# Strassen's seven products for five of eight pairs of contraction blocks in the feed-forward rounds of an encoder layer, in place of three

## The chip, the core and the metric

The kernel runs on one core of a Trainium2 chip. Five engines matter: TensorE (PE in the profile; its weight loads are PEld), VectorE (DVE), ScalarE (ACT), GpSimd (POOL) and SyncE (SP), whose queue issues the loads from memory. The metric is the device time of one execution in microseconds, lower is better. All data is 32-bit floating point.

## What is computed

One layer of an encoder on 256 tokens of width 2048: a feed-forward half, a mixing half (attention and a Fourier branch, gated), and a second feed-forward half. The change touches the two feed-forward halves alone:

```python
D_MODEL = 2048; SEQ = 256; D_FF = 5632

def _swiglu(x, w_gate, w_up, w_down):
    return (jax.nn.silu(x @ w_gate) * (x @ w_up)) @ w_down

def _macaron_ffn(x, pre_g, w_gate, w_up, w_down, post_g):
    return x + MACARON_WEIGHT * _rms_norm(_swiglu(_rms_norm(x, pre_g), w_gate, w_up, w_down), post_g)
...
    h = _macaron_ffn(h, ffn1_pre_g[l], ffn1_w_gate[l], ffn1_w_up[l], ffn1_w_down[l], ffn1_post_g[l])
    h = _gated_mixers(h, ...)
    h = _macaron_ffn(h, ffn2_pre_g[l], ffn2_w_gate[l], ffn2_w_up[l], ffn2_w_down[l], ffn2_post_g[l])
```

## The kernel before

**Precision by three products.** A 32-bit product is made of three passes of TensorE: every operand is split into a rounded part and its remainder. `split` (L102, L103) does that: ScalarE writes the rounded part `hi` by a copy, VectorE writes `lo = src - hi`. `mm3` (L107 to L109) then multiplies hi by hi, hi by lo and lo by hi into one PSUM tile. So each weight element that comes from memory costs ScalarE one element of copy, VectorE one of subtraction, and TensorE three passes for each of the two 128-token tiles.

**Rounds.** The 5632 columns of the feed-forward are 11 blocks of 512 (`f` = 0 to 10). The first two are made by `col_block`. For `f` = 2 to 10 there is one `swiglu` call each, 9 in each of the two halves, 18 in all: the gate and the up product of the block, both 256 x 512 with the 2048 contraction in 16 blocks of 128, that is 8 pairs of blocks. Between them stand the `row_line` calls, which multiply an earlier block's 256 x 512 result by `w_down` and add it to the row tiles `y` (two tiles of 128 x 2048, taken 512 columns at a time: `cb` = 0 to 3). A round, as the word is used here, is one `row_line` and the `swiglu` behind it.

**Strassen's form.** Seen as a 2 x 2 problem (two token tiles by gate and up, over a pair of contraction blocks), a pair costs eight block products, or seven by Strassen's way. A pair in the seven form needs sums of the token blocks (made once, in `Forms.chunk`) and sums of the weight blocks (made anew in every round, because the weights are new): in `seven`, four VectorE subtractions of 128 x 512 (`minus`, L538; two in `first`, then one in `first` behind a split, one in `second`). It feeds four pieces to TensorE: `rb` whole (2 products), `t` whole (2), `ra` whole (2), one half of `t` (1). A plain pair feeds two whole pieces (4 products each). In units of 128 x 1024 splits: 3.5 against 2. Each product is one `mm3`: 21 matmuls against 24. The products p1, p5, p6, p7 are common to several outputs and are added at the end by VectorE (`add`, L543) after ScalarE's `copy` (L547); then come `silu` (L551) and `times` (L555). In the kernel before, the three seven pairs are the first pairs of the first three chunks (`kg` = 0, 1, 2; a chunk is four contraction blocks), and the common products end with the third.

**Order.** The feed-forward rounds are scheduled by hand: VectorE, ScalarE and TensorE each keep program order. `Line.feed` keeps a queue of `RING` = 6 pieces: a piece's subtractions and split (`ready`) are issued when it enters, its matmuls (`use`) when six stand in the queue, and its additions (`then`) right behind its matmuls. So on VectorE a piece's additions stand ahead of the split of the sixth piece after it. The split pieces lie in a ring of six buffers, so the split of a piece waits until TensorE is done with the piece six before. Raw pieces (512 KB each) are loaded by SP's queue in order into `RAW_BUFS` = 5 buffers (L83); a load waits until its buffer's last reader is done.

**Buffers.** PSUM: five tiles `mm` (the accumulators u0, g0, g1, u1, p6, and two `pr` for each `cb` of a row line), three tiles `tr` (p1, p5, p7, and the transposes of `turn_h`, L177). `chunk` has three buffers under each of two names (the weight sums `t13`, and the transposed block results `hT`).

Of the kernel before, what the change touches and what calls it, by code (L numbers as in the profile page):

```python
# [10 lines left out]
F32 = mybir.dt.float32  # L11
# [37 lines left out]
BY_SEVEN = (0, 1, 2)  # L49
# [7 lines left out]
def encoder_layer(  # L57
# [371 lines left out]
    class Forms:  # L429
# [3 lines left out]
        def __init__(self, u, rs):  # L433
            self.u, self.rs, self.seven, self.plain = u, rs, {}, {}
            self.rooms = {}

        def room(self, n):

            for i, used in self.rooms.items():
                if used[0] + n <= D:  # L440
                    break
            else:
                i = len(self.rooms)
                used = self.rooms[i] = [0] + [big(f"f{c}{i}", F32R) for c in "hl"]
            used[0] += n
            return [a[:, used[0] - n:used[0]] for a in used[1:]]
# [11 lines left out]
        def chunk(self, kg):  # L458
# [6 lines left out]
            n = 0  # L465
            if kg in BY_SEVEN:
                n = 2
                f = chunk.tile([P, 7, P], F32, tag="ch_lo", name="sf")
                a11, a12, a21, a22 = a[:, 0, 0:P], a[:, 1, 0:P], a[:, 0, P:S], a[:, 1, P:S]
                A.activation(f[:, 0:2, :], a[:, 0:2, 0:P], AF.Copy)  # L470
                A.activation(f[:, 2, :], a22, AF.Copy, scale=-1.0)
                V.tensor_tensor(out=f[:, 3, :], in0=a21, in1=a22, op=ALU.add)
                V.tensor_tensor(out=f[:, 4, :], in0=f[:, 3, :], in1=a11, op=ALU.subtract)
                V.tensor_tensor(out=f[:, 5, :], in0=a11, in1=a21, op=ALU.subtract)
                V.tensor_tensor(out=f[:, 6, :], in0=a12, in1=f[:, 4, :], op=ALU.subtract)
                hi, lo = (x.rearrange("p (a b) -> p a b", b=P) for x in self.room(7 * P))
                split(hi, lo, f[:])
                self.seven[kg] = [(hi[:, i, :], lo[:, i, :]) for i in range(7)]
            hi, lo = (x.rearrange("p (a b) -> p a b", b=S) for x in self.room((CK - n) * S))
            split(hi, lo, a[:, n:, :])  # L480
            for k in range(n, CK):
                self.plain[kg * CK + k] = [(hi[:, k - n, t * P:(t + 1) * P], lo[:, k - n, t * P:(t + 1) * P]) for t in range(NT)]
# [35 lines left out]
    def swiglu(line, forms, w, hs):  # L518
# [10 lines left out]
        def plain(kg, i, c, ks, *then):  # L529
            def use(b):  # L530
                for t in range(NT):
                    for j, k in enumerate(ks):
                        mul(c + str(t), forms.plain[kg * CK + k][t], b[j], kg * CK + k == KD - 1)

            line.feed(lambda: ring(raw_piece(w[kg], i)[:]), use, *then)
# [22 lines left out]
        def seven(kg, end):  # L558
            a11, a12, na22, s1, s2, s3, s4 = forms.seven[kg]
            h = {}  # L560

            def first():
                ra, rb = raw_piece(w[kg], 0), raw_piece(w[kg], 1)
                t = chunk.tile([P, WP, NB], F32, tag=("ch_hi", "ch_lo")[kg % 2], name="t13")
# [12 lines left out]
            def two(n, a, m, b, last):  # L577
                def use(ws):
# [6 lines left out]
            plain(kg, 2, "g", (2, 3))  # L585
            line.feed(lambda: ring(h["ra"][:]), two("p1", a11, "p6", s2, end), *([copy, lambda: add("x2", "p6", "x1")] if end else []))
            line.feed(lambda: ring(h["t"][:, 0:1, :]), lambda ws: mul("g1", na22, ws[0]),
                      *([lambda: add("x3", "p7", "x2")] if end else []))
            plain(kg, 3, "u", (2, 3), *([lambda: add("x2", "p5", "x2")] if end else []))

        for kg in range(KD // CK):
            if kg in BY_SEVEN:
                seven(kg, kg == BY_SEVEN[-1])
                continue
            plain(kg, 0, "g", (0, 1), lambda: add("x5", "p5", "x3"))
            plain(kg, 1, "u", (0, 1))
            plain(kg, 2, "g", (2, 3), lambda: add("x1", "g0", "x1"), lambda: add("x3", "g1", "x3"),
                  lambda: silu(0), lambda: silu(1))
            plain(kg, 3, "u", (2, 3), lambda: add("x2", "u0", "x2"), lambda: times(0), lambda: add("x5", "u1", "x5"),
                  lambda: times(1))  # L600

    def row_line(line, ch, w, rb, y, first, ahead):

        for cb in range(D // NB):
            ps = []

            def use(b, i, cb=cb, ps=ps):
                if i == 0:
                    if cb == D // NB - 1:
                        ahead()  # L610
                    ps.extend(pmm.tile([P, NB], F32, tag="mm", name="pr") for _ in range(NT))
# [6 lines left out]
            def out(t, cb=cb, ps=ps):  # L618
                dst = cbs(y[t], cb)
                if first:  # L620
                    A.activation(dst, ps[t][:], AF.Copy)
                else:
                    V.tensor_tensor(out=dst, in0=ps[t][:], in1=dst, op=ALU.add)
# [5 lines left out]
    def ffn(u, rs, wg, wu, wgu, wd, yname, tail, gate0, w_next=None, early=()):  # L629
# [10 lines left out]
        for f in range(PLAIN):  # L640
# [19 lines left out]
        with tc.manual_schedule(engines={mybir.EngineType.DVE, mybir.EngineType.Activation, mybir.EngineType.PE}):  # L660
            for f in range(PLAIN, nblk + 1):
# [7 lines left out]
                row_line(line, chs[-1] if f > PLAIN else chs[0], wd, f - 2, y, f == PLAIN, ahead)  # L669
# [619 lines left out]
```

## Time and profile before

| | |
|---|---|
| median of three runs | 2040.54 us (2039.6 to 2041.2) |
| the profiled execution, its own time | 2041.46 us |
| its span from the first to the last instruction | 2039.7 us |
| TensorE busy | 2018.3 us, 99% of the span, 9308 matmuls |
| TensorE weight loads busy | 1673.0 us, 82% |
| VectorE busy | 1651.9 us, 81%, 2216 instructions |
| ScalarE busy | 1112.2 us, 55% |
| granted clock, mean | 0.999 of full speed |
| read from memory | 409.44 MB, 204 GB/s over the span |

A busy share is a mean over the whole span, and the feed-forward rounds are a regular stretch of it with shares of their own. A matmul of TensorE is counted from its start to its modelled end, and several are in flight at once, so its rate is read from the distance of two starts. The same holds for VectorE, where an instruction's end can lie behind the start of the next.

### The profile page before, as it was taken

The page shows a single profiled execution, that of the slowest core. Times are in us where ns is not written, and L with a number is a line of the kernel's source. Part 1 is how long each engine was busy: PE and PEld are TensorE (multiplying, and loading weights), DVE is VectorE, ACT ScalarE, POOL GpSimd, SP SyncE. Part 2 cuts the span into 40 slices and gives each one's busy share as a digit, 9 for nine tenths or more (in the row PEclk, how much of TensorE's full clock was granted, in tenths as well). Part 3 has the DMA queues.
Part 4 walks back from the last instruction along what each step waited for, and adds up shares of the span by engine and source line. Part 5 has one row for each costly group of instructions (what it writes and reads, how often), then busy time and mean ns, then how long its engine had stood idle before and what let it go on. Part 6 is the DMA issues. An engine that isn't in the chain of part 4 may idle for free.

```text
span 2039.7 us, 25718 instructions
## 1 busy us (share of the span) xinstructions
PE 2018.3 (99%) x9308; PEld 1673.0 (82%) x9308; DVE 1651.9 (81%) x2216; ACT 1112.2 (55%) x1490; POOL 50.9 (2%) x46
## 2 busy tenths in 40 slices
PE   9999999999999999999999999999999999999998
PEld 7888888888888878888888888788888888888886
DVE  6878888888888788887877895877788888888876
ACT  7554555544555556556666554555554555544553
POOL 0000000000000110100000000200000000000002
PEclk9999999999999999999999999999999999999999
DMA  8675566556666696964555557566665566656663
GB/s 315 212 271 178 190 218 205 193 175 201 209 207 190 208 294 194 271 187 138 192 190 188 183 179 276 186 207 225 220 203 173 192 218 204 196 174 198 211 209 106
DMA packets 118736, 417.43 MB, mean 205 GB/s; under 512 B 12968, under 2 KB 19120, under 8 KB 116432
## 3 DMA queue, kind: packets, MB, share of 16 engines
q1 hardware_dynamic: 114256, 411.66, 61.1%
q0 software_dynamic: 4352, 4.13, 1.4%
q8 instruction: 73, 1.20, 0.2%
q14 instruction: 55, 0.45, 0.1%
HBM read 409.44 MB, written 6.29 MB: 204 GB/s over the span
## 4 chain that ended last, share of the span: by engine, by line
PE 93%; DVE 4%; DMA 1%; ACT 1%; issue 0%; SPq 0%; DVEq 0%; ACTq 0%
PE pc L108 19%; PE pc L109 19%; PE pc L107 19%; PE pr L109 10%; PE pr L107 10%; PE pr L108 10%; PE pt L177 1%; DVE wlo L103 1%; DMA raw<-in_w_fo 1%; DVE h L390 0%; PE pe L107 0%; PE pe L109 0%; PE pe L108 0%; PE pt L976 0%; PE pf L109 0%
## 5 line engine op out<-in xcount | busy, mean ns | idle before, releaser
L102 ACT ACTIVATE whi<-raw 128x1024 fp32r<-128x1024 f32 (+1 forms) x711 | 749.0, 1059 | 618.8 <-PE pc L109 268.2
L103 DVE TENSOR_TENSOR wlo<-raw,whi 128x1024 fp32r<-128x1024 f32 (+1 forms) x711 | 860.5, 1220 | 277.1 <-ACT whi L102 271.4
L107 PE MATMUL pc<-whi,fh 128*128 128x512 f32 x1098 | 427.1, 389 | 0.0
L108 PE MATMUL pc<-wlo,fh 128*128 128x512 f32 x1098 | 427.1, 389 | 0.0
L109 PE MATMUL pc<-whi,fl 128*128 128x512 f32 x1098 | 427.1, 389 | 0.0
L107 PE MATMUL pc<-whi,uh 128*128 128x512 f32 x688 | 271.7, 395 | 0.2 <-ACT uh L698 0.2
L108 PE MATMUL pc<-wlo,uh 128*128 128x512 f32 x688 | 269.4, 392 | 2.3 <-DVE wlo L103 2.2
L109 PE MATMUL pc<-whi,ul 128*128 128x512 f32 x688 | 269.4, 392 | 1.5 <-DVE ul L103 1.5
L107 PE MATMUL pr<-whi,hTh 128*128 128x512 f32 x688 | 269.4, 392 | 0.0
L109 PE MATMUL pr<-whi,hTl 128*128 128x512 f32 x688 | 267.8, 389 | 0.0
L108 PE MATMUL pr<-wlo,hTh 128*128 128x512 f32 x688 | 267.7, 389 | 0.0
L107 PEld LDWEIGHTS pc<-whi,fh 128*128 128x128 f32 x1098 | 206.1, 188 | 42.8
L109 PEld LDWEIGHTS pc<-whi,fl 128*128 128x128 f32 x1098 | 206.1, 188 | 42.8
L108 PEld LDWEIGHTS pc<-wlo,fh 128*128 128x128 f32 x1098 | 206.1, 188 | 42.7
L109 PEld LDWEIGHTS pc<-whi,ul 128*128 128x128 f32 x688 | 129.4, 188 | 29.2 <-DVE ul L103 2.4
L108 PEld LDWEIGHTS pc<-wlo,uh 128*128 128x128 f32 x688 | 129.5, 188 | 28.9 <-DVE wlo L103 4.0
L107 PEld LDWEIGHTS pc<-whi,uh 128*128 128x128 f32 x688 | 129.5, 188 | 27.0 <-ACT uh L698 1.5
L109 PEld LDWEIGHTS pr<-whi,hTl 128*128 128x128 f32 x688 | 129.1, 188 | 26.9
L108 PEld LDWEIGHTS pr<-wlo,hTh 128*128 128x128 f32 x688 | 129.2, 188 | 26.1
L107 PEld LDWEIGHTS pr<-whi,hTh 128*128 128x128 f32 x688 | 129.2, 188 | 26.1
L102 ACT ACTIVATE whi<-t 128x1024 fp32r<-128x1024 f32 x108 | 90.9, 842 | 98.9 <-DVE t L538 44.5
L103 DVE TENSOR_TENSOR wlo<-t,whi 128x1024 fp32r<-128x1024 f32 x108 | 103.1, 954 | 15.6 <-ACT whi L102 15.6
(333 smaller groups left out, 2066.3 us busy)
## 6 DMA issues: line engine op xcount, KB each, us to landing
raw<-in_f_gu SPq DMA_DIRECT2D x288, 512.0 KB, 4.1
raw<-in_f_down SPq DMA_DIRECT2D x176, 512.0 KB, 5.0
raw<-in_w_in SPq DMA_DIRECT2D x112, 512.0 KB, 4.9
raw<-in_f_up SPq DMA_DIRECT2D x32, 512.0 KB, 4.7
raw<-in_w_ao SPq DMA_DIRECT2D x32, 512.0 KB, 4.0
raw<-in_w_out SPq DMA_DIRECT2D x32, 512.0 KB, 4.0
raw<-in_f_gate SPq DMA_DIRECT2D x31, 512.0 KB, 5.6
fraw<-in_w_f SPq DMA_DIRECT2D x16, 512.0 KB, 5.9
```

The lines of the kernel that those rows point to most:

```text
L102: a = A.activation(hi, src, AF.Copy)
L103: v = V.tensor_tensor(out=lo, in0=src, in1=hi.bitcast(F32), op=ALU.subtract)
L107: T.matmul(ps, lh, rh, start=first, stop=False)
L108: T.matmul(ps, lh, rl, start=False, stop=False)
L109: return T.matmul(ps, ll, rh, start=False, stop=last)
L177: T.transpose(pt[:, j, :], src[:, j * P:(j + 1) * P], ident[:])
```

## The change

Five pairs of the eight take the seven form: both pairs of the first chunk (0 and 1), and the first pair of the other three (2, 4 and 6). Pairs 3, 5 and 7 stay plain. With the last seven pair now in the last chunk, the common products are closed there, and their additions stand behind pair 6's third and fourth piece; the additions of gate and up stand behind the two pieces of pair 7 as they stood behind the last two pieces before. The order of the pieces in a round: in chunk 0 the eight pieces of two seven pairs; in chunks 1 and 2 the seven pair's first two, the plain pair's gate piece, the seven pair's other two, the plain pair's up piece; in chunk 3 the four of the seven pair, then the two of the plain one. The weights are laid out anew to fit. `put` replaces `room` and stores the same number of token blocks' splits in the same buffers. The last chunk's token forms (`forms.chunk(3)`) are made at the first piece of the first row line in place of in the block `f` = 1. `Y_BY_DMA` is off, so row tiles are added to `y` by VectorE as they were (`way` is "set" for the first row line, as `first` was, and "add" for the others).

```diff
-BY_SEVEN = (0, 1, 2)
+BY_SEVEN = (0, 1, 2, 4, 6)
+Y_BY_DMA = False
...
+        def put(self, src):
+
+            out, n = [], src.shape[1]
+            while len(out) < n:
+                if self.used == KD:
+                    self.rooms, self.used = [big("f" + c, F32R, [P, KD, P]) for c in "hl"], 0
+                a = len(out)
+                m = min(n - a, KD - self.used)
+                hi, lo = (r[:, self.used:self.used + m, :] for r in self.rooms)
+                split(hi, lo, src[:, a:a + m, :])
+                out += [(hi[:, i, :], lo[:, i, :]) for i in range(m)]
+                self.used += m
+            return out
...
+            for q in range(CK // 2):
+                pair = kg * CK // 2 + q
+                if pair in BY_SEVEN:
...
+                    self.seven[pair] = self.put(f[:])
+                else:
+                    four = self.put(a[:, 2 * q:2 * q + 2, :].rearrange("p k (t c) -> p (k t) c", t=NT))
+                    for i in range(2):
+                        self.plain[2 * pair + i] = four[NT * i:NT * i + NT]
...
+        def seven(pair, between=None, *then):
+            a11, a12, na22, s1, s2, s3, s4 = forms.seven[pair]
+            end = pair == BY_SEVEN[-1]
...
+                t = chunk.tile([P, WP, NB], F32, tag=("ch_hi", "ch_lo")[BY_SEVEN.index(pair) % 2], name="t13")
...
             line.feed(first, two("u0", s4, "g0", a12, False))
             line.feed(second, two("p5", s1, "p7", s3, end))
-            plain(kg, 2, "g", (2, 3))
-            line.feed(lambda: ring(h["ra"][:]), two("p1", a11, "p6", s2, end), *([copy, lambda: add("x2", "p6", "x1")] if end else []))
-            line.feed(lambda: ring(h["t"][:, 0:1, :]), lambda ws: mul("g1", na22, ws[0]),
-                      *([lambda: add("x3", "p7", "x2")] if end else []))
-            plain(kg, 3, "u", (2, 3), *([lambda: add("x2", "p5", "x2")] if end else []))
-
+            if between:
+                between()
+            line.feed(lambda: ring(h["ra"][:]), two("p1", a11, "p6", s2, end), *then[0:2])
+            line.feed(lambda: ring(h["t"][:, 0:1, :]), lambda ws: mul("g1", na22, ws[0]), *then[2:])
+
+        sums = [copy, lambda: add("x2", "p6", "x1"), lambda: add("x3", "p7", "x2"), lambda: add("x2", "p5", "x2"),
+                lambda: add("x5", "p5", "x3")]
+        gates = [lambda: add("x1", "g0", "x1"), lambda: add("x3", "g1", "x3"), lambda: silu(0), lambda: silu(1)]
+        ups = [lambda: add("x2", "u0", "x2"), lambda: times(0), lambda: add("x5", "u1", "x5"), lambda: times(1)]
         for kg in range(KD // CK):
-            if kg in BY_SEVEN:
-                seven(kg, kg == BY_SEVEN[-1])
-                continue
...
+            a, b = 2 * kg, 2 * kg + 1
+            if kg == KD // CK - 1:
+                seven(a, None, *sums)
+                plain(b, 0, *gates)
+                plain(b, 1, *ups)
+            elif b in BY_SEVEN:
+                seven(a)
+                seven(b)
+            else:
+                seven(a, lambda: plain(b, 0))
+                plain(b, 1)
...
-                pu = col_block(u, wu, f, between=[lambda: forms.chunk(2), lambda: forms.chunk(3)])
+                pu = col_block(u, wu, f, between=[lambda: forms.chunk(2)])
...
+                way = "set" if f == PLAIN else "dma" if Y_BY_DMA and f < nblk else "add"
+                before = {D // NB - 1: ahead}
+                if f == PLAIN:
+                    before[0] = lambda: forms.chunk(KD // CK - 1)
```

## Rows read from the trace of the kernel before

**Rows 1.** The page: busy time, share of the span and instructions of each engine.

```profile
PE 2018.3 (99%) x9308; PEld 1673.0 (82%) x9308; DVE 1651.9 (81%) x2216; ACT 1112.2 (55%) x1490; POOL 50.9 (2%) x46
```

**Rows 2.** The chain that ended last, in time order: start, duration, work; two transposes.

```profile
432.83 0.87 PE pt L177 x8
...
496.97 0.87 PE pt L177 x8
```

**Rows 3.** Busy time (and count) of each engine in that one round.

```profile
core 0: us, PE busy (x) PEld busy (x) DVE busy (x) ACT busy (x) POOL busy (x), PEclk, DMA share, GB/s
...
432.83:496.97 64.14, 64.14 (x290) 53.22 (x288) 53.36 (x63) 32.71 (x35) 0.00 (x0) 1.00 0.60 196
```

**Rows 4.** Timeline, TensorE: start, duration, instruction; thirteen matmuls in a row, first and last.

```profile
446.48 0.39 PE L107 MATMUL pc<-whi,fh 128*128 128x512 f32 x1
...
449.20 0.39 PE L107 MATMUL pc<-whi,fh 128*128 128x512 f32 x1
```

**Rows 5.** Groups by shape in the same round: count, busy, mean ns, idle before.

```profile
L103 DVE TENSOR_TENSOR wlo<-raw,whi 128x1024 fp32r<-128x1024 f32 x24 | 29.1, 1221 | 9.2 <-ACT whi L102 8.9
...
L107 PE MATMUL pc<-whi,fh 128*128 128x512 f32 x61 | 23.7, 389 | 0.0
...
L107 PE MATMUL pr<-whi,hTh 128*128 128x512 f32 x32 | 12.5, 392 | 0.0
...
L538 DVE TENSOR_TENSOR t<-raw 128x512 f32<-128x512 f32 x9 | 5.9, 687 | 0.1
L623 DVE TENSOR_TENSOR y<-pr,y 128x512 f32<-128x512 f32 x9 | 5.9, 684 | 0.7 <-PE pr L109 0.7
L543 DVE TENSOR_TENSOR x<-pc,x 128x512 f32<-128x512 f32 x8 | 5.4, 683 | 0.0
```

**Rows 6.** Timeline, VectorE: start, duration, instruction; one seven pair and a plain piece.

```profile
441.49 1.29 DVE L538 TENSOR_TENSOR t<-raw 128x512 f32<-128x512 f32 x2
442.69 1.22 DVE L103 TENSOR_TENSOR wlo<-raw,whi 128x1024 fp32r<-128x1024 f32 x1
443.82 0.69 DVE L538 TENSOR_TENSOR raw<-raw,t 128x512 f32<-128x512 f32 x1
444.42 1.22 DVE L103 TENSOR_TENSOR wlo<-t,whi 128x1024 fp32r<-128x1024 f32 x1
445.68 0.69 DVE L538 TENSOR_TENSOR t<-raw 128x512 f32<-128x512 f32 x1
446.29 2.35 DVE L103 TENSOR_TENSOR wlo<-raw,whi 128x1024 fp32r<-128x1024 f32 x2
448.56 0.69 DVE L103 TENSOR_TENSOR wlo<-t,whi 128x512 fp32r<-128x512 f32 x1
```

**Rows 7.** Timeline at a round's end, VectorE, then ScalarE; idle before in brackets.

```profile
477.48 1.28 DVE L543 TENSOR_TENSOR x<-pc,x 128x512 f32<-128x512 f32 x2
480.41 1.23 DVE L103 TENSOR_TENSOR wlo<-raw,whi 128x1024 fp32r<-128x1024 f32 x1 [1.65 <-ACT whi L102]
...
478.19 1.23 ACT L551 ACTIVATE x<-x 128x512 f32<-128x512 f32 x2 [1.89 <-DVE x L543]
```

**Rows 8.** Waits in the same round: total us, times, longest.

```profile
ACT whi L102 <- PE pr L109: 12.0, 7, 2.1
DVE wlo L103 <- ACT whi L102: 9.7, 10, 1.6
```

**Rows 9.** Line L83: three loads' issues (timeline of SP), the last two's landing.

```profile
451.80 0.33 SPq L83 DMA_DIRECT2D raw<-in_f_gu  x1
...
456.63 0.33 SPq L83 DMA_DIRECT2D raw<-in_f_gu  x1
...
DMA to landing us min/median/max: 3.5/3.5/3.5
...
457.74 0.33 SPq L83 DMA_DIRECT2D raw<-in_f_gu  x1
...
DMA to landing us min/median/max: 5.0/5.0/5.0
```

**Rows 10.** Timeline, VectorE, in the first row line of the first half.

```profile
102.88 1.23 DVE L103 TENSOR_TENSOR wlo<-raw,whi 128x1024 fp32r<-128x1024 f32 x1 [1.93 <-ACT whi L102]
```

More of the change, by code (lines that the diff above doesn't have):

```diff
@@ L464, in chunk @@
             V.tensor_tensor(out=a[:], in0=a[:], in1=self.r[:].unsqueeze(1).to_broadcast([P, CK, S]), op=ALU.mult)
-            n = 0
-            if kg in BY_SEVEN:
[L467 to L482, printed above, removed]
+            for q in range(CK // 2):
+                pair = kg * CK // 2 + q
+                if pair in BY_SEVEN:
+                    f = chunk.tile([P, 7, P], F32, tag="ch_lo", name="sf")
+                    k0, k1 = 2 * q, 2 * q + 1
+                    a11, a12, a21, a22 = a[:, k0, 0:P], a[:, k1, 0:P], a[:, k0, P:S], a[:, k1, P:S]
+                    A.activation(f[:, 0:2, :], a[:, k0:k1 + 1, 0:P], AF.Copy)
+                    A.activation(f[:, 2, :], a22, AF.Copy, scale=-1.0)
+                    V.tensor_tensor(out=f[:, 3, :], in0=a21, in1=a22, op=ALU.add)
+                    V.tensor_tensor(out=f[:, 4, :], in0=f[:, 3, :], in1=a11, op=ALU.subtract)
+                    V.tensor_tensor(out=f[:, 5, :], in0=a11, in1=a21, op=ALU.subtract)
+                    V.tensor_tensor(out=f[:, 6, :], in0=a12, in1=f[:, 4, :], op=ALU.subtract)
+                    self.seven[pair] = self.put(f[:])
[3 more added lines that the diff above has]
+                        self.plain[2 * pair + i] = four[NT * i:NT * i + NT]
@@ L527, in mul, with raw, plain @@
             begun.add(n)
-        def plain(kg, i, c, ks, *then):
+        def raw(pair, i):
+            return raw_piece(w[pair // 2], pair % 2 * 2 + i)
+        def plain(pair, i, *then):
             def use(b):
                 for t in range(NT):
-                    for j, k in enumerate(ks):
-                        mul(c + str(t), forms.plain[kg * CK + k][t], b[j], kg * CK + k == KD - 1)
-            line.feed(lambda: ring(raw_piece(w[kg], i)[:]), use, *then)
+                    for j in range(2):
+                        k = 2 * pair + j
+                        mul("gu"[i] + str(t), forms.plain[k][t], b[j], k == KD - 1)
+            line.feed(lambda: ring(raw(pair, i)[:]), use, *then)
         def minus(out, a, b):
@@ L556, in times @@
             hs.append(up)
-        def seven(kg, end):
-            a11, a12, na22, s1, s2, s3, s4 = forms.seven[kg]
+        def seven(pair, between=None, *then):
+            a11, a12, na22, s1, s2, s3, s4 = forms.seven[pair]
+            end = pair == BY_SEVEN[-1]
             h = {}
             def first():
-                ra, rb = raw_piece(w[kg], 0), raw_piece(w[kg], 1)
-                t = chunk.tile([P, WP, NB], F32, tag=("ch_hi", "ch_lo")[kg % 2], name="t13")
+                ra, rb = raw(pair, 0), raw(pair, 1)
+                t = chunk.tile([P, WP, NB], F32, tag=("ch_hi", "ch_lo")[BY_SEVEN.index(pair) % 2], name="t13")
                 h.update(ra=ra, rb=rb, t=t)
@@ L608, in use @@
                 if i == 0:
-                    if cb == D // NB - 1:
-                        ahead()
+                    if cb in ahead:
+                        ahead[cb]()
                     ps.extend(pmm.tile([P, NB], F32, tag="mm", name="pr") for _ in range(NT))
@@ L619, in out @@
                 dst = cbs(y[t], cb)
-                if first:
+                if way == "set":
                     A.activation(dst, ps[t][:], AF.Copy)
+                elif way == "dma":
+                    part = work("part")
+                    A.activation(part[:], ps[t][:], AF.Copy)
+                    nc.gpsimd.dma_start(dst, part[:], accum_op=ALU.add)
                 else:
```

35 lines of the change are left out of this document (9 added, 26 removed).

## The prediction, made before the changed kernel ran

> **What bounds the kernel now.** First the engines' shares on the page: TensorE is busy for 99% of the span, VectorE for 81%, ScalarE for 55% [rows 1]. Then the chain of work that ended last: in the feed-forward it is matmuls only, and the transposes of the block result mark the rounds, from 432.83 to 496.97 us, so a round lasts 64.14 us [rows 2]. The busy times of that one round say how far the other engines are from it: VectorE 53.36 us, ScalarE 32.71, TensorE the whole 64.14, at full clock (1.00, the 2.4 GHz level), the DMA engines at 0.60 [rows 3]. A matmul is shown as 0.39 us long, but twelve of them start within 449.20 - 446.48 = 2.72 us, so one costs 0.2267 us [rows 4]. A round has 3 x 61 = 183 gate and up matmuls and 3 x 32 = 96 of the row line [rows 5]; 279 x 0.2267 + 0.87 for the transposes [rows 2] = 64.12 us. The sum closes: TensorE never waits in a round, and only fewer matmuls can shorten it, as long as VectorE keeps up.
>
> **What the change removes.** A pair in the seven form has 21 matmuls in place of 24. Two more pairs save 6 a round: 6 x 0.2267 = 1.36 us, and TensorE's round falls to 62.76 us. There are 18 such rounds, so at most 24.5 us are to be had.
>
> **What it adds on VectorE.** Shown durations overlap, so costs go from start to start. Two 512-wide subtractions take 442.69 - 441.49 = 1.20, so 0.60 each; a split of 1024 takes 443.82 - 442.69 = 1.13, and two in a row (448.56 - 446.29)/2 = 1.135; the split whose source the next subtraction overwrites takes 445.68 - 444.42 = 1.26 [rows 6]. A whole seven pair is 1.20 + 1.13 + 0.60 + 1.26 + 0.61 + 1.135 + 0.62 = 6.55 us (the last, the half piece, taken as a 512-wide subtraction); a plain pair is 2 x 1.135 = 2.27. Two pairs changed over add 2 x 4.28 = 8.56 us a round. On ScalarE they add 3 splits a round, about 3 us; it has 32.71 of 64.14 in use [rows 3], and this costs nothing.
>
> A round's ledger after the change, in us. The 512-wide additions from PSUM (sums, `y`) are as long as those from SBUF (684 and 683 ns against 687) [rows 5], so 0.60 each as well.
>
> - Row line: TensorE 96 x 0.2267 + 0.87 = 22.6; VectorE 8 splits 9.1, 8 additions to `y` 4.8, 2 splits of the transposes 1.2: 15.1.
> - Pairs 0 and 1, both seven: TensorE 42 matmuls 9.5; VectorE 13.1.
> - Pairs 2 and 3, and again 4 and 5: TensorE 45 matmuls 10.2; VectorE 8.8, each.
> - Pairs 6 and 7: TensorE 10.2; VectorE 8.8 and ten 512-wide additions and products at the end 6.0, with 0.2 for those that follow on their own input: 15.0.
>
> TensorE 62.8, VectorE 60.9. One wait of VectorE can't be filled: at the round's end the two gate additions start at 477.48, ScalarE does its two SiLU behind them from 478.19 and only then the next piece's copy, and VectorE's split starts at 480.41, after 1.65 us of nothing [rows 7]. The new order has the same chain in the same place. 60.9 + 1.7 = 62.6 us: VectorE is level with TensorE. The other idle time of the round, above all the 9.7 us in which VectorE waited for ScalarE's copy while that waited for TensorE to free a ring buffer [rows 8], is the cover that the 8.56 us use up.
>
> **Which wait comes then.** Level totals mean that VectorE falls behind and catches up within a round. It loses 3.6 us in pairs 0 and 1 and 4.8 us in pairs 6 and 7, and gains 7.5 in the row line and 1.4 in each of the other pairs. The six pieces of the ring are about 16 us of TensorE's time in the row line and 7 us in a stretch of seven pieces, so the dips by themselves fit. While VectorE catches up, it no longer waits for TensorE but for the raw buffers: a load can start only when the reader of the piece five before is done. Take a leader, a load issued after a quiet stretch (456.63, 4.8 us behind the one at 451.80): it landed in 3.5 us; the one right behind it, at 457.74, took 5.0 [rows 9].
>
> - The second raw piece of pairs 4 and 6 takes the buffer that pair 2's (4's) second piece leaves. VectorE has 1.135 + 1.135 + 0.62 + 1.135 + 0.60 = 4.6 us of other work in between. These loads come some 5 us after the one before, so they are leaders: 3.5 + 0.1 fits.
> - The row line's second piece takes pair 6's second buffer, likewise a leader: five splits, 5.15 us, against 3.6 and ScalarE's copy of 1.1: fits.
> - The third follows 1.1 us later, with 5.0 to land and 1.2 for issue and copy: 6.2 + 1.1 = 7.3 us after the first was issued, and VectorE comes for it after 5.15 + 1.135 + 0.60 = 6.9. It waits about 0.5 us.
>
> VectorE's round is then 62.6 + 0.5 = 63.1 us, and TensorE goes at that pace, with its stalls where the lead runs out, behind pairs 0 and 1. Bounds of this wait: nothing (a landing of 4.5) to 0.9 (5.4).
>
> **Edits with one answer.** The common products keep p1, p5, p6, p7 in PSUM until pair 6. The next row line needs two `mm` tiles: p6's, free after pair 6's third piece, and g0's, whose addition may come up to 2.5 us behind TensorE if VectorE is late; but only the row line's seventh matmul needs it (1.4 us in), so the bound is 0 to 1 us a round and I take 0. What stands behind these additions on VectorE are the row line's splits, and they have a lead of 5 pieces. `forms.chunk(3)` moves to the first row line, once in each half: at most some 6.5 us of VectorE's time there, where ScalarE writes `y` in place of 4.8 us of additions, and where VectorE waited (1.93 us ahead of one split alone [rows 10]); 0, at most 2 us a half. The loads keep their number and size. `Y_BY_DMA` is off and costs nothing.
>
> **The sum.** 64.13 - 63.14 = 0.99 us x 18 = 17.8 us. The profiled execution took 2041.46 us around a span of 2039.7, and the median is 2040.54; the saving is taken from the median: 2022.7, say 2023 us.
>
> **A rule against it.** The trace starts a VectorE instruction before the end that it shows for the one ahead: two of 0.69 are done in 1.29, two of 1.22 in 2.35 [rows 6]. The Trainium skill, page "VectorE: DVE Perf Modes", section "The DRAIN you can't avoid", says that after every operation the pipe is emptied before the next starts, and refers to another section for the ones that start earlier. By the first rule a round's VectorE time would be the sum of the shown durations. Here the trace disagrees with it, by 0.09 us an instruction, and where this kernel would go if full durations held is the third rival.
>
> **The rivals.**
>
> 1. *All of it arrives.* If the followers land in 4.6 us or less, VectorE's round is 62.6 and TensorE's 62.76 sets the pace: 2040.5 - 24.5 = 2016. For it: VectorE kept its lead everywhere before. Against: 0.2 us of slack in 63.
> 2. *The raw buffers turn into the bound* (slower). If the leaders too land in 5.0 us, as followers do [rows 9], pairs 4 and 6 each wait 5.2 + 1.1 - 5.2 = about 1.0 us (load, then copy, against 4.6 + 0.6 of VectorE's work) and the row line's second piece 5.2 + 1.1 - 5.15 = 1.1; the third then waits no more. 62.6 + 3.2 = 65.8 us: 1.7 x 18 = 30 us more, 2070. It decides from a landing of about 4.4 us for these three loads, where the round reaches 64.1. For it: in a tight train no load is quiet for long. Against: the 4.8 us before each of them.
> 3. *Full durations.* 29 splits x 1.22 + 45 others x 0.69 + 1.7 = 68.1 us a round: + 4.0 x 18 = 72 us, 2112. Against: [rows 6], throughout.
> 4. *It cancels out.* VectorE's waits come to 1.5 us a round more than its 62.6 (a VectorE 2% slower than its row while ScalarE and the loads run beside it would do): 64.1, no change. That the change does not do what it says, with matmuls unchanged, would end here too; the diff speaks against it.
>
> **How the numbers follow.** Forecast 0.58, rival 1 0.19, rival 2 0.12, rival 3 0.02, rival 4 0.09. A measurement of this kernel tells about 0.2%, 4 us, from no change. Faster by more: forecast and rival 1, 0.77. Same: 0.09. Slower: 0.14. The range goes from rival 1 less 0.5 us of spread, 2015.5, up to 2037, where the waits take 1.2 of the 1.36 us; beyond lie rivals 2 to 4. About 0.78 lie within.
>
> **What would show it.** Right: the transposes 62.8 to 63.9 us apart; some 177 gate and up matmuls a round; VectorE busy for about 98% of a round; TensorE's first waits on `lo` in pairs 1 and 2, some tenths of a us each; a wait of ScalarE's copy for a load in the row line. Wrong: VectorE waiting for `raw` in pairs 4 and 6 (rival 2), TensorE without waits (rival 1), or waits of `pr` for a PSUM tile. The step most likely to fail is that landing times stay as they are when the loads are bunched anew.

## The result, and the profile after

| | before | after |
|---|---|---|
| median | 2040.24 us (2039.6 to 2041.2, 4 runs) | 2029.88 us (2027.47 to 2032.05, 4 runs) |
| ratio, with 95% interval | | 0.9949 [0.9931, 0.9966] |
| the profiled execution, span | 2041.46, 2039.7 us | 2027.47, 2025.7 us |

The change makes the kernel faster by 10.4 us; 2023 was forecast, in a range of 2015.5 to 2037. The direction and the range held, and the gain is three fifths of the 17.5 us between the forecast and 2040.5.

The page's first part (busy time, share of the span, instructions), and under "..." its summary of the chain that ended last:

```profile
PE 1999.5 (99%) x9200; PEld 1649.6 (81%) x9200; DVE 1796.7 (89%) x2452; ACT 1162.6 (57%) x1574; POOL 51.1 (3%) x46
...
PE 66%; DVE 27%; issue 2%; DMA 2%; ACT 2%; SPq 0%; DVEq 0%; ACTq 0%
```

Against [rows 1], TensorE has 108 matmuls less, which is 18 rounds x 6, and VectorE 236 instructions more. The second line is the news: before, the chain ran on TensorE for 93% and on VectorE for 4%; now more than a quarter of it is VectorE's. TensorE is still shown busy for 99% of the span, so the busy shares alone don't tell of it.

The round of [rows 3], three times: one early and one late in the first half, and the longest of the second half (stretch, its length, then busy time and count of each engine, granted clock, DMA share, GB/s):

```profile
core 0: us, PE busy (x) PEld busy (x) DVE busy (x) ACT busy (x) POOL busy (x), PEclk, DMA share, GB/s
174.31:237.17 62.86, 62.86 (x283) 51.99 (x282) 60.94 (x75) 35.34 (x39) 0.00 (x0) 1.00 0.60 201
489.34:552.65 63.31, 63.12 (x283) 51.93 (x281) 61.10 (x75) 35.41 (x39) 0.00 (x0) 1.00 0.59 200
1603.80:1668.89 65.09, 63.50 (x283) 51.83 (x281) 60.91 (x75) 35.07 (x39) 0.00 (x0) 1.00 0.60 194
```

VectorE's busy time is the same in all three, 60.9 to 61.1 us, and so is the number of its instructions. What grows from the first to the last is time in which it stands idle: 1.9, 2.2 and 4.2 us. All 18 rounds, from transposes to transposes: in the first half 62.79, 62.86, 62.85, 62.88, 62.98, 63.46, 63.31, 63.23, 63.52 us; in the second 62.79, 63.94, 63.50, 65.09, 63.62, 64.19, 63.58, 63.47, 63.55. Before, each took 64.13 to 64.15. The rounds together give 12.8 of the 14.0 us by which the span is shorter. At 62.79 each they would have given 24.2; 11.4 us were lost on the way.

**Where VectorE stands idle.** At two places, some 50 and 44 us into a round, where it splits the first pieces of the row line (timeline of VectorE in two rounds: start, duration, instruction, in brackets the idle time before it and who ended it):

```profile
473.48 1.28 DVE L550 TENSOR_TENSOR x<-pc,x 128x512 f32<-128x512 f32 x2
476.41 1.23 DVE L104 TENSOR_TENSOR wlo<-raw,whi 128x1024 fp32r<-128x1024 f32 x1 [1.65 <-ACT whi L103]
...
1513.82 4.69 DVE L104 TENSOR_TENSOR wlo<-raw,whi 128x1024 fp32r<-128x1024 f32 x4
1518.42 0.69 DVE L550 TENSOR_TENSOR x<-pc,x 128x512 f32<-128x512 f32 x1
1520.47 1.23 DVE L104 TENSOR_TENSOR wlo<-raw,whi 128x1024 fp32r<-128x1024 f32 x1 [1.36 <-ACT whi L103]
```

The first two lines are the SiLU chain of [rows 7], 1.65 us as before, and it comes in every round. The second wait is new. The copy that it waits for was itself waiting for a load (timeline of ScalarE, then on SP's queue the issue of the load ahead of that one, called the leader as in the prediction, and of that load, the follower, each with its time from issue to landing):

```profile
1519.38 1.06 ACT L103 ACTIVATE whi<-raw 128x1024 fp32r<-128x1024 f32 x1 [1.65 <-DMA raw<-in_f_down]
...
1512.14 0.33 SPq L84 DMA_DIRECT2D raw<-in_f_down  x1
...
DMA to landing us min/median/max: 3.5/3.5/3.5
...
1513.24 0.33 SPq L84 DMA_DIRECT2D raw<-in_f_down  x1
...
DMA to landing us min/median/max: 6.0/6.0/6.0
```

The leader landed in 3.5 us, the follower issued 1.1 us behind it in 6.0. The wait in this place was between 0 and 0.6 us in the first half, 1.6 us over its nine rounds, and up to 1.4 us in the second, 6.5 us there: 8.2 of the 11.4 us. Two others, 1.08 and 0.26 us, make it 9.5 us of waiting beside the SiLU chain. (The first round of each half, which TensorE sets with 62.79 us, has some more waits, and they cost nothing there.)

**Who then waits for VectorE.** ScalarE with the SiLU, and TensorE through its weight loads (PEld) in two ways (waits over the whole span: total us, times, longest):

```profile
ACT x L558 <- DVE x L550: 58.5, 18, 3.7
...
PEld pc L109 <- DVE wlo L104: 14.5, 29, 1.5
...
PEld pr L108 <- DVE x L550: 4.3, 5, 1.8
```

The first line is the SiLU waiting for its addition, once in each of the 18 rounds. The second is TensorE at a piece whose low half isn't split yet; before, the like came to 4.0 us over the span, and every round kept to 64.13 to 64.15. The third is the row line without a PSUM tile, since the gate addition that frees it is late.

### The profile page after: what moved, and what is told of

It is laid out like the page before. It is cut to its first block, busy times and chain, and to the rows that moved or that the text cites. A ratio compares the mean times of both kernels' runs of the same rounds, so it can differ in the third digit from the quotient of the medians.

```text
span 2025.7 us, 25877 instructions
## 1 busy us (share of the span) xinstructions
PE 1999.5 (99%) x9200; PEld 1649.6 (81%) x9200; DVE 1796.7 (89%) x2452; ACT 1162.6 (57%) x1574; POOL 51.1 (3%) x46
## 3 DMA queue, kind: packets, MB, share of 16 engines
q8 instruction: 72, 1.18, 0.2%
## 4 chain that ended last, share of the span: by engine, by line
PE 66%; DVE 27%; issue 2%; DMA 2%; ACT 2%; SPq 0%; DVEq 0%; ACTq 0%
PE pc L109 14%; PE pc L110 14%; PE pc L108 14%; DVE wlo L104 14%; PE pr L108 6%; PE pr L110 6%; PE pr L109 6%; DVE t L545 4%; DVE yf L640 2%; DVE raw L545 1%; DVE x L550 1%; ACT whi L103 1%; DVE y L640 1%; PE pt L178 1%; DVE hTl L104 1%
## 5 line engine op out<-in xcount | busy, mean ns | idle before, releaser
L103 ACT ACTIVATE whi<-raw 128x1024 fp32r<-128x1024 f32 (+1 forms) x711 | 739.1, 1055 | 408.6 <-PE pc L110 118.1
L109 PE MATMUL pc<-wlo,fh 128*128 128x512 f32 x1062 | 415.8, 392 | 2.0 <-DVE wlo L104 1.8
L108 PE MATMUL pc<-whi,fh 128*128 128x512 f32 x1062 | 413.4, 389 | 0.0
L110 PE MATMUL pc<-whi,fl 128*128 128x512 f32 x1062 | 413.3, 389 | 0.0
L103 ACT ACTIVATE whi<-t 128x1024 fp32r<-128x1024 f32 (+1 forms) x180 | 152.6, 848 | 221.1 <-DVE t L545 200.3
L109 PEld LDWEIGHTS pc<-wlo,fh 128*128 128x128 f32 x1062 | 199.3, 188 | 51.5 <-DVE wlo L104 10.8
L108 PEld LDWEIGHTS pc<-whi,fh 128*128 128x128 f32 x1062 | 199.3, 188 | 41.7
L110 PEld LDWEIGHTS pc<-whi,fl 128*128 128x128 f32 x1062 | 199.4, 188 | 40.7
L545 DVE TENSOR_TENSOR t<-raw 128x512 f32<-128x512 f32 x270 | 178.0, 687 | 3.1
L104 DVE TENSOR_TENSOR wlo<-t,whi 128x1024 fp32r<-128x1024 f32 (+1 forms) x180 | 171.2, 951 | 2.7 <-ACT whi L103 2.7
```

What stands on the lines that cost most here:

```text
L103: a = A.activation(hi, src, AF.Copy)
L104: v = V.tensor_tensor(out=lo, in0=src, in1=hi.bitcast(F32), op=ALU.subtract)
L108: T.matmul(ps, lh, rh, start=first, stop=False)
L109: T.matmul(ps, lh, rl, start=False, stop=False)
L110: return T.matmul(ps, ll, rh, start=False, stop=last)
L545: V.tensor_tensor(out=out, in0=a, in1=b, op=ALU.subtract)
```

## The experiments

Three theories were put against each other. *Theory 1*: the round is now VectorE's; its work (61.2 us), the SiLU chain (1.65) and the load wait stand one behind the other, and less of any of the three shortens it. *Theory 2*: VectorE has slack, and the late loads alone, with too few raw buffers, cost the 11 us. *Theory 3*: TensorE stalls since PSUM tiles are held until late gate additions. The experiments are given in the order of these questions. Times stand beside 2029.9 us for the changed kernel, and ratios are to the kernel before, run beside each experiment.

### One more subtraction a round, in the changed kernel and in the one before

```diff
                 minus(ra[:, 1, :], rb[:, 0, :], t[:, 0, :])
+                if pair == 0:
+                    minus(ra[:, 1, :], rb[:, 0, :], t[:, 0, :])
                 return b
```

In the kernel before the condition is `kg == 0`.

> The changed kernel with one more 512-wide subtraction of VectorE in each round (pair 0's last subtraction is done twice, the output is the same). Theory 1, VectorE's own pace is the round (61.2 us of work, 1.65 us behind the SiLU, and a wait for a load): each round grows by the whole 0.60 us, 17 to 18 times, so about 10 us more than the changed kernel's 2029.9: 2038 to 2041, and the rounds that now last 62.8 us grow too. Theory 2, VectorE has slack and only the wait for the raw loads takes the gain back: the 0.60 us goes into slack, at most 3 us more. Theory 3, TensorE waits for PSUM tiles that late gate additions hold: pair 0 is far from them, 0 to 3 us more.

> The kernel before with the same extra 512-wide subtraction in each round that cost the changed kernel 12 us (first seven pair, done twice; the output is the same). Theory 1: before, VectorE waited 9.7 us a round for TensorE to free ring buffers, so 0.60 us disappears in that and the round stays at 64.13: within 1 us of 2040.5. Theory 2 and 3 say the same; if an extra subtraction costs 10 us here too, the 12 us are not VectorE's pace but a cost of the instruction itself, and theory 1 falls.

The changed kernel with it took 2041.99 us (2039.48 to 2044.7), ratio 1.0007 [0.9998, 1.0015]: 12.1 us for 18 subtractions, 0.67 us each, and the whole gain is gone. That is 1 us above what theory 1 foresaw, and the first round of each half, which theory 1 had growing too, stayed at 62.8 us. The kernel before with it took 2040.1 us, ratio 0.9996 [0.9987, 1.0005]: nothing. One round of each (columns as above; the changed one first):

```profile
367.67:432.21 64.54, 63.92 (x283) 51.76 (x282) 61.72 (x77) 35.27 (x40) 0.00 (x0) 1.00 0.59 196
```

```profile
367.95:432.09 64.14, 64.14 (x289) 53.20 (x288) 53.95 (x64) 32.69 (x35) 0.00 (x0) 1.00 0.61 197
```

The same instruction costs its full length where VectorE idles for 2.8 us of the round and nothing where it idles for 10.2. So 2.8 us of idle time in the changed kernel are no slack: nothing can be put into them, since they are waits that stand in VectorE's own order. Theory 2, which gives VectorE slack, falls; so does theory 3 as the only cause, which had at most 3 us for it.

### Four pairs in place of five

```diff
-BY_SEVEN = (0, 1, 2, 4, 6)
+BY_SEVEN = (0, 2, 4, 6)
```

> The changed kernel with four pairs in the seven form (0, 2, 4, 6), pair 1 plain. TensorE has three matmuls more a round: 62.79 + 0.68 = 63.47 us; VectorE 4.3 us less: 56.9 + 1.65 = 58.6. Theory 1: VectorE is out of the way, every round lasts 63.47 and there is no spread: 2040.2 - 18 x 0.66 = 2028.3, no slower than five pairs, which would say that the fifth pair's 0.68 us a round brought nothing. Theory 2: the order of loads at a round's end is the same as with five pairs, so the waits stay and it comes to 2028 + 9 = 2037. Theory 3: as theory 2, if the gate additions are late for reasons other than VectorE's load.

2028.15 us (2027.58 to 2029.1), ratio 0.9938 [0.9926, 0.9951], and every round 63.45 to 63.48 us. Its busy times (columns as above), then two waits of VectorE in the round:

```profile
365.68:429.13 63.45, 63.45 (x286) 52.63 (x285) 57.16 (x69) 34.07 (x37) 0.00 (x0) 1.00 0.62 199
...
383.77 1.23 DVE L104 TENSOR_TENSOR wlo<-raw,whi 128x1024 fp32r<-128x1024 f32 x1 [1.30 <-ACT whi L103]
...
415.76 1.23 DVE L104 TENSOR_TENSOR wlo<-raw,whi 128x1024 fp32r<-128x1024 f32 x1 [1.65 <-ACT whi L103]
```

The SiLU chain's 1.65 us is here too, but TensorE works through all of the 63.45 us; VectorE has 4 us fewer to do, and its waits cost nothing. The fourth pair brought all that its three matmuls promise, 0.68 us a round. The fifth brought nothing that can be told from zero: the median with five pairs is 1.7 us above that with four, but the runs overlap, and both profiled spans are 2025.7 us. Three more matmuls were saved, and VectorE's waits took them.

### The SiLU behind the next piece

ScalarE runs its instructions in order, and the two SiLU stood ahead of the next piece's copy. Here they are issued one piece later, with that piece's additions; the products then come last.

```diff
-        gates = [lambda: add("x1", "g0", "x1"), lambda: add("x3", "g1", "x3"), lambda: silu(0), lambda: silu(1)]
-        ups = [lambda: add("x2", "u0", "x2"), lambda: times(0), lambda: add("x5", "u1", "x5"), lambda: times(1)]
+        gates = [lambda: add("x1", "g0", "x1"), lambda: add("x3", "g1", "x3")]
+        ups = [lambda: silu(0), lambda: silu(1), lambda: add("x2", "u0", "x2"), lambda: add("x5", "u1", "x5"),
+               lambda: times(0), lambda: times(1)]
```

> The changed kernel with the two SiLU moved one piece later, behind pair 7's up piece, so that ScalarE's copy of the next piece no longer stands behind them. Theory 1: the 1.65 us in which VectorE has nothing to do at a round's end go, its round falls to 61.2 + 0.3 for the products that now wait a little + 0.5 for loads = 62.0, below TensorE's 62.79, so the rounds go to 62.8 to 63.0: 2017 to 2021. Theory 2: no gain, since VectorE only comes earlier to the same loads: 2028 to 2031. Theory 3: the gate additions come earlier by 1.65 us in the following round, and the PSUM waits (1.4 us in one round seen) go: 2026 to 2029.

2016.16 us (2015.98 to 2016.95), ratio 0.9879 [0.9866, 0.9893]. This is 14 us faster than the changed kernel and the lowest median of all that ran, a little below the 2017 to 2021 of theory 1. Theory 2 foresaw no gain and theory 3 at most 4 us, so neither is the cause alone. A round, then on VectorE the place of the chain and a later wait, then the SiLU on ScalarE:

```profile
300.00:362.78 62.78, 62.78 (x283) 52.07 (x282) 60.80 (x75) 35.81 (x39) 0.00 (x0) 1.00 0.61 201
...
472.14 1.28 DVE L550 TENSOR_TENSOR x<-pc,x 128x512 f32<-128x512 f32 x2
473.33 1.22 DVE L104 TENSOR_TENSOR wlo<-raw,whi 128x1024 fp32r<-128x1024 f32 x1
474.47 1.28 DVE L550 TENSOR_TENSOR x<-pc,x 128x512 f32<-128x512 f32 x2
...
493.62 1.23 DVE L104 TENSOR_TENSOR wlo<-raw,whi 128x1024 fp32r<-128x1024 f32 x1 [0.73 <-ACT whi L103]
...
472.86 1.23 ACT L558 ACTIVATE x<-x 128x512 f32<-128x512 f32 x2 [1.54 <-DVE x L550]
```

The SiLU still waits for its addition, but the copy has gone ahead, and VectorE's split follows the additions at once. VectorE's work is the same to 0.2 us, with the same instructions, and all rounds last 62.77 to 62.79 us: TensorE's own time. The 1.65 us of waiting was the difference between an engine that sets the pace and one that keeps up. The load waits have gone with it, with no buffer added, but for three of 0.25 to 0.37 us in the second half that cost nothing. What idle time is left stands mostly early in the round (0.73 us at 493.62), where ScalarE's copies around that one wait for TensorE to free the ring; for that one the profile names nobody.

### The SiLU later, and two more subtractions

The edit just shown, and the duplicate subtraction under `if pair in (0, 2)`.

> The kernel with the SiLU moved one piece later (2016.2 us), with two extra 512-wide subtractions a round (pairs 0 and 2, done twice; the output is the same). Theory 1: there VectorE idles 1.1 to 1.4 us of a 62.77 us round, all of it waits that it could fill, so 1.20 us more use the slack up and some waits for loads come out again: 62.8 to 63.5 a round, 2017 to 2029. If the slack were larger than that (TensorE alone the bound), 2016; if the extra work counts in full, 2016 + 21.6 = 2038.

2025.91 us (2025.06 to 2030.21), ratio 0.9931 [0.9914, 0.9948], rounds of 62.84 to 63.81. Two subtractions are 1.2 us, near what the move had set free, and the waits are back (VectorE, 44 us into a round of 63.76; then TensorE's weight loads over the whole span: total us, times, longest):

```profile
408.50 1.23 DVE L104 TENSOR_TENSOR wlo<-raw,whi 128x1024 fp32r<-128x1024 f32 x1 [1.33 <-ACT whi L103]
...
PEld pc L109 <- DVE wlo L104: 8.3, 20, 1.5
...
PEld pr L108 <- DVE x L550: 9.0, 14, 1.0
```

Together with the first experiment this is theory 1 from both sides: work can stand in for the chain's wait. Work is 61.2 + 1.2 = 62.4 us here, the wait behind the SiLU is gone, and with the wait for the load the sum passes TensorE's 62.8: in the round shown 62.4 + 1.33 = 63.7.

### A raw buffer of its own for the load that is late

The second raw piece of the row line takes a buffer of the chunk pool, so that the load behind it no longer follows so closely.

```diff
-    def raw_piece(src, i):
-        raw = wraw.tile([P, WP, NB], F32, tag="raw", name="raw")
+    def raw_piece(src, i, aside=False):
+        raw = (chunk.tile([P, WP, NB], F32, tag="ch_lo", name="raw") if aside
+               else wraw.tile([P, WP, NB], F32, tag="raw", name="raw"))
...
-                line.feed(lambda i=i, cb=cb: ring(raw_piece(w[rb, cb], i)[:]), lambda b, i=i, use=use: use(b, i),
+                line.feed(lambda i=i, cb=cb: ring(raw_piece(w[rb, cb], i, way != "set" and (cb, i) == (0, 1))[:]),
+                          lambda b, i=i, use=use: use(b, i),
```

> The changed kernel with the raw buffer of the row line's second piece taken from the chunk buffers, which stand free there, so that the five raw buffers carry one piece less and the third piece's load starts 1.1 us earlier and as a leader. Theory 1: VectorE's wait ahead of that third piece (0 to 2.3 us a round, 9.5 us in sum over the profiled execution) goes, its round is 62.85 and TensorE's 62.79: 2040.2 - 18 x 1.28 = 2017, to 2021 if the waits move to another piece in part. Theory 2: the same 2017 to 2021. Theory 3: nothing, 2028 to 2031.

2023.89 us (2022.63 to 2026.97), ratio 0.992 [0.9907, 0.9934]: 6.0 us less than the changed kernel, where up to 9.5 were to be had, and slower than the 2017 to 2021 that theories 1 and 2 both foresaw. One round, and the two waits of TensorE's weight loads over the span:

```profile
362.86:425.77 62.91, 62.91 (x282) 52.00 (x281) 60.99 (x75) 35.31 (x39) 0.00 (x0) 1.00 0.61 201
...
PEld pc L109 <- DVE wlo L104: 11.1, 26, 1.4
...
PEld pr L108 <- DVE x L551: 0.4, 2, 0.2
```

The first half's rounds are now 62.8 to 62.91 us but for one of 63.18, VectorE's pace without a load wait. In the second half five of the nine still take 63.2 to 63.6: 0.48 us of waiting has turned up at another load, the second raw piece of the last seven pair, 33 us into the round. This is the place that rival 2 named. So the load wait was a cause, as theory 2 has it too, but not alone, and a buffer moves part of it to another load.

### Both: the SiLU later and the buffer

> The SiLU one piece later and the row line's second raw piece in a chunk buffer, both. With the SiLU alone the rounds lasted 62.77 us, TensorE's own time. Theory 1: TensorE is the bound there, so freeing the loads too brings nothing: 2015.5 to 2017.5. If loads still held the rounds up, 2010 to 2014.

2016.87 us (2015.44 to 2019.75), ratio 0.9887 [0.9873, 0.9902], rounds of 62.77 to 62.80. The buffer adds nothing that shows once VectorE keeps up. In this order of the pairs the load wait is thus no bound of its own but a consequence of VectorE's lost lead.

### Row tiles added to `y` by DMA

```diff
-Y_BY_DMA = False
+Y_BY_DMA = True
```

> The changed kernel with its switch for adding row tiles to y set the other way: in the row lines of blocks 3 to 10 ScalarE copies the PSUM tile and a DMA of GpSimd's queue adds it to y, so VectorE has eight additions, 4.8 us, less a round and ScalarE 4.6 us more. Theory 1: VectorE 56.4 + 1.65 = 58 us, far below TensorE's 62.79, so all of the matmuls' gain comes out: 2015 to 2019, unless the adding DMAs (2 MB a round beside 12.5 MB of weights, read and written) hold the weight loads up. Theory 2: the waits for raw loads stay or grow, 2030 or more. Theory 3: PSUM tiles are freed by ScalarE, 2016 to 2020.

2018.84 us (2018.01 to 2020.27), ratio 0.989 [0.9875, 0.9905]. A round, and the adding DMAs of the whole span (count, KB of each, median us from issue to landing):

```profile
362.59:425.37 62.78, 62.78 (x283) 52.09 (x282) 56.44 (x67) 39.86 (x47) 6.88 (x8) 1.00 0.78 231
...
y<-part POOLq DMA_DIRECT2D x64, 256.0 KB, 6.5
```

Eight additions of a round leave VectorE, 4.6 us of busy time, and the round is TensorE's again. This is another way to take VectorE off the path, at 0.78 of the DMA engines' time in place of 0.60. It ends 2.7 us behind the moved SiLU. Of the 2.9 us between the two profiled spans some 0.5 lie in the rounds and the rest between the two halves, where this run's granted clock is 0.79 from 720 to 728 us and the other's is 1.00 throughout; whether that accounts for all of it is open.

### The fifth pair in the third chunk

```diff
-BY_SEVEN = (0, 1, 2, 4, 6)
+BY_SEVEN = (0, 2, 4, 5, 6)
```

> The changed kernel with the five seven pairs at 0, 2, 4, 5, 6: the stretch of two seven pairs in a row stands in the third chunk in place of the first, straight ahead of pair 6 and its sums. Work of all engines is the same. Theory 1: VectorE is the bound over the whole round, so where its load is bunched does not matter: 62.85 and the wait for loads, 2027 to 2033. If the depth of the dip against the ring decides (the lead of six pieces runs out because 13.1 us, 8.8 and 15.0 of VectorE's work follow each other with no row line between them), it is slower: 2035 to 2045.

2062.14 us (2059.59 to 2065.11), ratio 1.0102 [1.0087, 1.0117]: slower than before the change, with as many instructions on each engine, and none of the ranges foreseen had this number. Its waits of TensorE's weight loads for a PSUM tile over the span:

```profile
PEld pr L108 <- DVE x L550: 40.3, 18, 3.2
```

In all 18 rounds, 2.2 us each on average, the row line's second tile is still held by the gate product whose addition VectorE hasn't done. The matmuls behind these weight loads start after 1.1 to 2.8 us of idle time, 32.7 us in all. One of them, on TensorE:

```profile
487.49 0.39 PE L110 MATMUL pr<-whi,hTl 128*128 128x512 f32 x1
...
490.31 0.80 PE L108 MATMUL pr<-whi,hTh 128*128 128x512 f32 x1 [2.44 <-DVE x L550]
490.91 0.63 PE L109 MATMUL pr<-wlo,hTh 128*128 128x512 f32 x1
491.33 0.63 PE L110 MATMUL pr<-whi,hTl 128*128 128x512 f32 x1
```

And VectorE in the same round: a wait early on, then one 4 us ahead of the additions, then the additions:

```profile
457.77 1.23 DVE L104 TENSOR_TENSOR wlo<-raw,whi 128x1024 fp32r<-128x1024 f32 x1 [1.03 <-ACT whi L103]
...
485.38 1.23 DVE L104 TENSOR_TENSOR wlo<-raw,whi 128x1024 fp32r<-128x1024 f32 x1 [1.54 <-ACT whi L103]
...
489.57 1.28 DVE L550 TENSOR_TENSOR x<-pc,x 128x512 f32<-128x512 f32 x2
```

Three seven pairs in a row end right ahead of the round's additions, so VectorE is at its latest when the PSUM tiles are due. The second wait, 1.54 us here and 15.8 us over the 18 rounds, is again one for a load (ScalarE's copy ahead of it waited 2.09 us for `raw`), and it delays the additions in turn: in 15 of the 18 rounds TensorE's idle time is 0.90 to 0.92 us longer than this wait, here 2.44 against 1.54. So the dip alone goes with some 0.9 us a round and the load with about as much. A kernel of this order with the spare raw buffer, which would part the two, did not run. Earlier, 18 us into the round, it idles for 1.03 us where the copies next to that one wait for TensorE to free the ring: its lead ends at the ring's size and can't be saved up for later. This is theory 3, which in the changed kernel was worth 4.3 us in 5 waits of the weight loads.

### The same, with the SiLU later

> The seven pairs moved (0, 2, 4, 5, 6) and the SiLU one piece later, both. With the pairs moved alone TensorE waited 1.3 to 2.6 us in each round ahead of the row line's second PSUM tile, for the gate additions, and VectorE idled 1.0 to 1.3 us where the ring was full. If the pace of VectorE over the round decides (theory 1 alone), taking 1.65 us of its idle time away gives 2016 to 2022. If the dip does (VectorE starts it with the ring full, as far ahead as it can be, and loses 3.6 and 4.8 us in one go until the gate additions are late), the 1.65 us only lengthen its idle time at the full ring, TensorE's wait for the PSUM tile stays, and it is 2040 to 2062.

2062.5 us (2056.68 to 2062.85), ratio 1.01 [1.0083, 1.0117]. The wait for the PSUM tile is as it was (whole span):

```profile
PEld pr L108 <- DVE x L550: 41.6, 18, 2.8
```

What was worth 14 us in one order of the pairs is worth nothing in the other: there the bound is the dip in VectorE's lead within the round, with the load wait that comes in it, and not VectorE's total. The load wait is 0.4 to 1.5 us in all but two of these rounds too, and in most of them TensorE again idles for 0.9 us more than that.

## Why the prediction was right, and where its size was off

**TensorE's saving.** Right. 62.76 us a round was forecast, and the rounds without a wait take 62.79; 177 gate and up matmuls, 108 fewer in all.

**VectorE's ledger: the term that was mis-sized.** Right in its make-up, and to half a per cent in size: 60.9 us of work forecast, 61.2 measured (62.85 - 1.65 in rounds with no other wait). The SiLU wait was forecast from one row as the wait that can't be filled, and it was 1.65 us in every round. The pace 62.6 was thus 0.25 us short, and since VectorE sets the pace nothing takes that up: 4.5 us in 18 rounds. The ledger's rule, costs from start to start, holds again. The groups of one round:

```profile
L104 DVE TENSOR_TENSOR wlo<-raw,whi 128x1024 fp32r<-128x1024 f32 x24 | 28.8, 1219 | 1.9 <-ACT whi L103 1.9
...
L109 PE MATMUL pc<-wlo,fh 128*128 128x512 f32 x59 | 23.1, 392 | 0.2 <-DVE wlo L104 0.2
...
L545 DVE TENSOR_TENSOR t<-raw 128x512 f32<-128x512 f32 x15 | 9.9, 687 | 0.2
```

29 splits at 1.22 us, which is 35.4, and 45 others at 0.69, 31.1, would be 66.4 us by full durations, and 68.1 with the SiLU wait; a round took 62.86. Rival 3 is out. By the first rule of the Trainium skill, "VectorE: DVE Perf Modes", section "The DRAIN you can't avoid", each of these instructions would empty the pipe ahead of the next; the trace (62.86 against 68.1) disagrees, as it did before the change. The section itself refers to another one for a next instruction that starts earlier.

**The third piece's load.** The place was right, and so was the formula: landing + 1.2 for issue and copy + 1.1 for the later issue, less VectorE's 6.9. At the 6.0 us that the follower took in the round shown, it gives 6.0 + 1.2 + 1.1 - 6.9 = 1.4, and 1.36 was measured; it comes within 0.15 us in 15 of the 16 rounds that follow the first of each half. But the landing was taken as 5.0 from a single row [rows 9], with bounds of 4.5 to 5.4 (at 5.0 the formula gives 0.4, and the forecast took 0.5). It came to 4.3 to 5.3 us in the first half and 4.7 to 6.0 in the second, and in four of the second half's nine rounds the wait was above its bound of 0.9 us. Forecast were 0.5 x 18 = 9 us of it in all; measured were 8.2. The size was right on the whole and in no half, 1.6 us in one and 6.5 in the other, so that the total fits is luck. Why the loads of the second half land later is open.

**What the sum had left out.** In the profiled execution, 18 rounds x (63.42 - 63.14) = 5.0 us are missing. VectorE's pace gives 4.5 of them. The waits on top of it come to 63.42 - 62.85 = 0.57 us a round against 63.14 - 62.6 = 0.54, so the rest of it is half a microsecond: less at the load than forecast, 1.3 us at the two other places, and 0.8 that has no row of its own. The five waits for a PSUM tile, 4.3 us by the profile, were taken as 0 in the forecast, and it named them as a sign of being wrong, which thus came. They lie inside the same delay, since they are waits for a VectorE that is late already: the longest round, with the longest of them, is 61.2 of work and 1.65 + 1.08 + 1.18 of VectorE's waits, 65.1 us, and took 65.09. The median is 2.4 us above the profiled execution, which is the shortest of four that lie 4.6 us apart; what differs in the longer ones no trace here shows.

**Edits put at nothing.** The moved `forms.chunk(3)` has no cost that shows: outside the 18 rounds the profiled span is 1.2 us shorter than before. The leaders ahead of the row line landed in 3.1 to 3.8 us in the second half, where the trace tells it, against a forecast of 3.5, and in the changed kernel VectorE waits for no load of pairs 4 and 6. (The 1.08 us in the longest round were for a piece of pair 5, whose load, a follower, took 7.5 us.) Rival 2, which needed 4.4 us for the leaders, did not come.

**TensorE's waits.** First behind pairs 0 and 1, as forecast. 19.4 us after the transposes of one round:

```profile
508.75 0.50 PE L109 MATMUL pc<-wlo,fh 128*128 128x512 f32 x1 [0.18 <-DVE wlo L104]
```

The second to the fourth round of the first half have no load wait: there the third piece's load landed in 4.3, 4.5 and 4.7 us, near the 4.6 that rival 1 asked for. But they last 62.85 to 62.88 us, which is VectorE's pace with the SiLU wait and not TensorE's 62.79. Of the signs named, the transposes were to be 62.8 to 63.9 us apart; three rounds are longer, up to 65.09.

**Dips.** "The dips by themselves fit" was right for this order of the pairs, and the margin was thin. With the fifth pair in the third chunk, the term for the PSUM tiles, bounded at 1 us and taken as 0, is 1.1 to 2.8 us of idle TensorE in every round, about half of it with the load wait.

**What the prediction didn't say.** It named the SiLU wait as 1.65 us that can't be filled, and took it as given. The experiments show that it decides over the whole change: with it the fifth pair is worth nothing that shows, without it the kernel reaches 2016 us, the forecast of rival 1.

## What to carry to other kernels

Before work is given to an engine with idle time, count its work and those of its waits that stand in its own order and can't be filled: 61 of 63 us and one chain of 1.65 was already a full engine, though its share of the span was 89%. Look for the head of such a chain in the queue of another engine (here two SiLU ahead of an independent copy), and move that first; here it was worth 14 us, beside the 10 of the change as it stood. And where two engines are level, the order within the round counts as much as the totals: heavy pieces belong well ahead of the point at which others wait for the engine's results, not right before it.

## What the hardware showed that was not expected

**A stall that can take the clock with it.** In the kernel with the fifth pair in the third chunk, TensorE idled for 2.44 us up to 490.31, and the matmuls after it started 491.33 - 490.91 = 0.42 us apart, against 0.227 in [rows 4]. Three stretches of that round, then the whole of another, with a stall of 2.65 us (columns as above):

```profile
439.68:489.00 49.32, 48.19 (x217) 39.69 (x215) 46.55 (x56) 27.32 (x30) 0.00 (x0) 1.00 0.59 199
489.00:496.00 7.00, 5.69 (x18) 4.57 (x19) 5.29 (x8) 4.10 (x5) 0.00 (x0) 0.76 0.48 141
496.00:506.72 10.72, 10.72 (x49) 8.85 (x48) 10.69 (x14) 4.25 (x4) 0.00 (x0) 1.00 0.54 172
...
1437.95:1503.69 65.74, 63.09 (x283) 52.01 (x281) 57.57 (x70) 36.86 (x42) 0.00 (x0) 1.00 0.64 218
```

The granted clock is 1.00 (2.4 GHz) up to the stall, 0.76 over the 7 us around it, a part of them at the lower level of 1.2 GHz, and 1.00 again afterwards. The three longest rounds of that kernel, 66.8 to 67.4 us, have such a stretch, behind stalls of 2.08 to 2.81 us; the other fifteen have none, though one of them stalled for 2.65 us. So the length of the stall alone does not decide. Where the clock fell, a stall cost more than its own length: without it that round lasts 67.05 - 2.44 = 64.6 us, the other 65.74 - 2.65 = 63.1. In the changed kernel TensorE idled for 1.4 us at most within a round, and from 100 to 2000 us its granted clock is 1.00.

**The same load, 3.1 to 7.5 us.** In the changed kernel's rounds, loads of one size and one queue landed in 3.1 to 3.9 us when issued 4 us or more behind the one ahead (but for one of 5.8, the first of the second half), and in 3.9 to 7.5 us when issued some 1.1 us behind it. Five buffers hide the former and not always the latter.
